# Where the weight tiles of 256-column products begin: 8 bytes instead of 64 behind a multiple of 512

## The chip, the cores and the metric

The kernel runs on one core of a Trainium2 chip. The metric is the time of one execution on the device in microseconds (us), the median of several runs. The engines are named as in the profile: PE is TensorE's matmul, PEld its weight load (which may run beside a matmul), DVE is VectorE, ACT is ScalarE, POOL is GpSimd, SP is SyncE.

## The reference

Two pre-norm residual layers over 512 tokens and 1024 channels, each with a mixer and a gated feed-forward block, all modulated by a conditioning vector; then a last norm. Everything is float32.

```python
for i in range(2):
    shift, scale, gate = adaln_params(c, ada_w[i, 0], ada_b[i, 0])
    hn = rmsnorm(h, norm_g[i, 0]) * (1.0 + scale) + shift
    m = s5_mixer(hn, ...) if i == 0 else fox_mixer(hn, ...)   # state space; causal attention, 16 heads
    h = h + gate * m
    shift, scale, gate = adaln_params(c, ada_w[i, 1], ada_b[i, 1])
    hn = rmsnorm(h, norm_g[i, 1]) * (1.0 + scale) + shift
    a, b = jnp.split(hn @ w_up, 2, axis=-1)                   # 1024 -> 2 x 2816
    h = h + gate * ((jax.nn.silu(causal_conv3(a)) * b) @ w_down)
return rmsnorm(h, final_g)
```

## The kernel before, in words

Channels lie on the 128 partitions and tokens along the free dimension, so a product multiplies a stationary 128x128 weight tile with a moving block of activations of up to 512 columns (tokens).

Each large product is done in three passes of a reduced float32 format. A value is split into a high part, rounded to that format, and the low rest (`put_parts`: ScalarE writes `w_hi`, VectorE subtracts and writes `w_lo`). `mms` (its matmul is lines 294 and 295) multiplies hi by hi, hi by lo and lo by hi into one PSUM sum. Every one of the three loads its 128x128 weights anew.

`product` handles a list of output tiles in up to three stages:

- `head`: the first tiles at once. For the two feed-forward layers it works in two halves of 256 tokens (`HALVES`), so that the first half can begin while the norm of the second is under way. The output product of the attention has a head too, with `halves=(slice(0, S),)`, one pass of 512.
- the middle: one output tile after the other over all 512 tokens.
- `tail`: the last 2 or 4 tiles again in halves of 256 tokens, so that the next norm's statistics of the first half can begin early. Tails stand in the state-space output product (moving `zhi`, `zlo`), both feed-forward down products (`ghi`, `glo`) and the attention's output product (`v`).

`quarters` makes most pairs of up-projection tiles by a scheme with seven products of half size instead of eight. Its inner function `times` (line 550) issues 4 x 3 matmuls of 256 columns for each of the seven, 84 for a pair, and 33 pairs in all. VectorE forms the sums of weight blocks (`sums`, line 518), `parts` splits them, and ScalarE and VectorE put the products together (`nm_h` line 557, `nm_t` line 518). Between pairs come pieces of the down product of the group before, over 512 columns on line 294.

Weight tiles come from `part_of`: a tile with 128 elements more than needed, whose contents begin `aside` elements behind the start. The pools are padded (`fill`) so that tiles begin at multiples of 512 bytes in a partition, and the 128x128 pieces of a tile are 512 bytes apart: what `aside` sets holds for every piece. Before, `aside` was 0 by default (heads, middles) and `ASIDE = 16` elements, 64 bytes, for tails, quarter products and the value products of the attention. In the value products (`fox_values`, matmul on line 1361) the weights are the moving operand and the activations the stationary one.

The order on each engine is that of the program text with a few added constraints; weight loads come over SyncE's queue, and a background task of the modulation weights (`ada_units`) uses POOL's queue and VectorE (line 247) during the first feed-forward layer.

Of the kernel before, what the change touches and what calls it, by code (L numbers as in the profile page):

```python
# [17 lines left out]
P = 128  # L18
# [40 lines left out]
def fill(pool, n):  # L59

    pool.tile([P, n // 4], F32, name="fill", bufs=1)


ROOM, ASIDE = 9 * P, 16


def part_of(pool, shape, name, tag, bufs, aside=0):
# [6 lines left out]
class Trunk:  # L74
# [223 lines left out]
    def product(self, w, ms, nk, x, evac, head=0, tail=0, after=None, ticks=0, halves=HALVES, tail_pool=(), first=None, step=None):  # L298


        ms = list(ms)
        full = slice(0, S)
        if head:
            wk = first or {m: self.weights(w[m], nk) for m in ms[:head]}
            ps = {m: self.mm.tile([P, S], F32, name="mmp") for m in ms[:head]}
            for c in halves:
                for k in range(nk):
                    for m in ms[:head]:
                        self.mms(ps[m][:, c], wk[m], x, k, nk, c)
                    self.finish_norm((k + 1) * head)  # L310
                    if step:
                        step(3)
            for m in ms[:head]:
                evac(m, ps[m], full)
                self.tick(ticks)
        for m in ms[head:len(ms) - tail]:
            wk = self.weights(w[m], nk)
            ps = self.mm.tile([P, S], F32, name="mmp")
            for k in range(nk):
                self.mms(ps, wk, x, k, nk, full)  # L320
                if step:
                    step()
            evac(m, ps, full)
            self.tick(ticks)
        if tail:
            last = ms[len(ms) - tail:]
            wk = {m: self.weights(w[m], nk, *tail_pool, aside=ASIDE) for m in last}
            for c in HALVES:
                for m in last:
                    if c is HALVES[1] and m == last[tail // 2]:  # L330
                        rb = self.rms_rows(y)
                    ps = self.mm.tile([P, S // 2], F32, name="mmp")
                    for k in range(nk):
                        self.mms(ps, wk[m], x, k, nk, c)
                    evac(m, ps, c)
                if c is HALVES[0]:
                    y = after[0](c)
                else:
                    y2 = after[0](c)
                    after[1](HALVES[0], y, rb)  # L340
            self.pending = lambda: after[1](HALVES[1], y2)
# [947 lines left out]
class Kernel(S5):  # L1289
# [32 lines left out]
    def fox_values(self, pool, x):  # L1322

        nc = self.nc

        self.v = pool.tile([P, KT, NB, 2, 2, HD], F32R, name="v")
        ft = pool.tile([P, NB, NH], F32, name="ft")
        fill(pool, 1792)
        bf = self.fox_bf
        W = VH * HD  # L1330
        xhi, xlo = x

        def load(qs):

            out = {q: [] for q in qs}
            for c in range(3):
                for q in qs:
                    src = self.io["fox_v"][q - 1] if q else self.io["fox_vf"]
                    n, step = (W, 4) if q else (W + NH, 3)
                    a = c * step  # L1340
                    j = min(step, KT - a)
                    if j <= 0:
                        continue
                    with self.behind(*(self.squared if 0 in qs and c else ())):
                        hi, lo = self.split(src[:, a:a + j, :], [P, j, n], aside=ASIDE)
                    out[q] += [(hi[:, i, :], lo[:, i, :]) for i in range(j)]
            return out

        def values(qs, blocks, w, aux=()):
            todo = [(q, b) for q in qs for b in blocks]  # L1350
            ps = {
                k: self.aux.tile([P, S], F32, name="aux") if k in aux else self.mm.tile([P, S], F32, name="mmp")
                for k in todo
            }
            for k in range(KT):
                for q, b in todo:
                    hi, lo = w[q][k]
                    n = W if q else W + NH
                    tb = slice(b * P, (b + 1) * P)
                    for i, (xt, wt) in enumerate(((xhi, hi), (xhi, lo), (xlo, hi))):  # L1360
                        self.last_mm = nc.tensor.matmul(  # L1361
                            ps[q, b][:, :n], xt[:, k, tb], wt, start=(k == 0 and i == 0), stop=(k == KT - 1 and i == 2),
                        )
                self.finish_norm((k + 1) * len(todo))
            for q, b in todo:
                pv = ps[q, b][:, :W].rearrange("p (g r d) -> p g r d", r=2, d=HD)
                hi, lo = (self.v[:, 2 * q:2 * q + 2, b, :, t, :] for t in range(2))
                self.evac = [self.put_parts(hi, lo, pv).ins]
                if todo[0][0] == 0 and (b != 1 or q):
                    self.tick(1)  # L1370
                if q == 0:
                    nc.vector.tensor_tensor(ft[:, b, :], ps[q, b][:, W:W + NH], bf, ALU.add)

        w = load(range(2))
        self.tick(1)
        values((0, 1), (0, 1), w)
        values((0, 1), (2, 3), w, ((0, 2), (0, 3)))
        lf = self.log_forget(ft, pool)
        for q in range(2, NV):
            values((q,), range(NB), load([q]))  # L1380
        return lf
# [259 lines left out]
```

## Time and profile before

| | |
|---|---|
| median of 3 runs | 1240.85 us (1239.77 to 1241.22) |
| profiled execution | 1233.09 us, span of its instructions 1231.3 us |
| granted TensorE clock | 0.995 of full speed |
| PE busy | 1200.5 us, 7921 matmuls |
| PEld busy | 1031.2 us, 7921 loads |
| DVE busy | 1009.0 us, 1872 instructions |
| ACT busy | 606.3 us, 1137 instructions |
| bytes moved by DMA | 183.83 MB |

The durations of matmuls are those of a pipelined engine: one may begin before the one before it has ended, so the time that a run of matmuls takes is read from the distance between starts. A row of a stretch gives for each engine the busy time in it and, in brackets, how many instructions began there.

### The profile page before, as it was taken

How to read it: one execution, taken by the hardware profiler on the slowest of the kernel's cores; microseconds unless marked ns; L12 is line 12 of the kernel's file. 1: busy time of each engine (PE TensorE's matmuls, PEld its weight loads, DVE VectorE, ACT ScalarE, POOL GpSimd, SP SyncE). 2: the span in 40 equal slices, each digit the busy share in tenths (PEclk: the TensorE clock that was granted, in tenths of full speed). 3: DMA queues.
4: the chain of work that ended last, by engine and by line, in shares of the span. 5: the costliest groups of instructions: out<-in, count | busy, mean ns of one | idle time of the engine just before them, and what ended most of it. 6: DMA issues, size and time to landing. Idle time of an engine off the chain costs nothing.

```text
span 1231.3 us, 20566 instructions
## 1 busy us (share of the span) xinstructions
PE 1200.5 (97%) x7921; PEld 1031.2 (84%) x7921; DVE 1009.0 (82%) x1872; ACT 606.3 (49%) x1137; POOL 82.7 (7%) x143
## 2 busy tenths in 40 slices
PE   7999999999999999999999999999999999999997
PEld 2466678898989899889899887878989999999987
DVE  7988886779899988799687578876899887888865
ACT  3543465335544543445443565664366554545443
POOL 0000000100000000000000243430000000000000
PEclk9999999999999999999999999999999999999999
DMA  9776668530354544444445543432122332323231
GB/s 356 244 237 215 223 225 286 192 129 35 129 178 158 192 161 160 152 168 132 125 139 190 176 150 124 147 118 94 70 69 95 120 122 77 116 86 123 95 96 69
DMA packets 74385, 183.83 MB, mean 149 GB/s; under 512 B 23231, under 2 KB 25631, under 8 KB 73263
## 3 DMA queue, kind: packets, MB, share of 16 engines
q1 hardware_dynamic: 68239, 161.02, 38.4%
q0 software_dynamic: 5760, 20.97, 5.0%
q8 instruction: 62, 1.02, 0.3%
q10 hardware_dynamic: 288, 0.52, 0.1%
q14 instruction: 36, 0.29, 0.1%
HBM read 175.57 MB, written 6.92 MB: 148 GB/s over the span
## 4 chain that ended last, share of the span: by engine, by line
PE 75%; DVE 15%; DMA 4%; issue 3%; ACT 2%; POOL 0%; SPq 0%; DVEq 0%; ACTq 0%; POOLq 0%
PE mmp L294 32%; PE mmp L550 16%; PE aux L550 6%; DVE w_lo L278 5%; PE mmp L1169 4%; PE mmp L1361 2%; DMA rawd<-in_w_down 2%; PE aux L971 2%; PE mmp L1198 2%; PE aux L1060 1%; PE aux L1500 1%; PE mmp L205 1%; PE aux L1052 1%; DVE ada_raw L247 1%; PE mmp L1109 1%
## 5 line engine op out<-in xcount | busy, mean ns | idle before, releaser
L278 DVE TENSOR_TENSOR w_lo<-raw,w_hi 128x1024 fp32r<-128x1024 f32 (+4 forms) x173 | 183.3, 1065 | 35.4 <-ACT w_hi L277 34.8
L277 ACT ACTIVATE w_hi<-raw 128x1024 fp32r<-128x1024 f32 (+4 forms) x173 | 154.8, 905 | 101.5 <-PE mmp L294 53.1
L294 PE MATMUL mmp<-ghi,w_hi 128*128 128x512 f32 (+1 forms) x392 | 145.1, 370 | 0.0
L294 PE MATMUL mmp<-glo,w_hi 128*128 128x512 f32 (+1 forms) x392 | 144.8, 369 | 0.0
L294 PE MATMUL mmp<-ghi,w_lo 128*128 128x512 f32 (+1 forms) x392 | 144.5, 369 | 0.0
L294 PE MATMUL mmp<-a_hi,w_hi 128*128 128x512 f32 (+1 forms) x376 | 138.8, 372 | 1.5 <-ACT a_hi L433 1.5
L294 PE MATMUL mmp<-a_hi,w_lo 128*128 128x512 f32 (+1 forms) x376 | 136.6, 364 | 0.3 <-DVE w_lo L278 0.3
L294 PE MATMUL mmp<-a_lo,w_hi 128*128 128x512 f32 (+1 forms) x376 | 136.2, 363 | 0.0
L550 PE MATMUL mmp<-w_hi 128*128 128x256 f32 x396 | 111.4, 281 | 2.6 <-ACT nm_h L557 2.6
L550 PE MATMUL mmp<-w_hi,w_lo 128*128 128x256 f32 x396 | 111.1, 281 | 0.7 <-DVE w_lo L278 0.7
L550 PE MATMUL mmp<-w_lo,w_hi 128*128 128x256 f32 x396 | 111.1, 281 | 0.0
L557 ACT ACTIVATE nm_h<-mmp 128x256 f32<-128x256 f32 x99 | 37.9, 384 | 131.5 <-PE mmp L550 131.5
L278 DVE TENSOR_TENSOR w_lo<-sums,w_hi 128x1024 fp32r<-128x1024 f32 x74 | 90.1, 1219 | 0.3 <-ACT w_hi L277 0.2
L294 PEld LDWEIGHTS mmp<-ghi,w_lo 128*128 128x128 f32 x392 | 74.2, 189 | 12.7 <-DVE w_lo L278 0.4
L294 PEld LDWEIGHTS mmp<-glo,w_hi 128*128 128x128 f32 x392 | 74.5, 190 | 11.1
L277 ACT ACTIVATE w_hi<-sums 128x1024 fp32r<-128x1024 f32 x74 | 76.7, 1054 | 14.4 <-DVE sums L518 11.2
L294 PEld LDWEIGHTS mmp<-ghi,w_hi 128*128 128x128 f32 x392 | 74.2, 189 | 11.4
L294 PEld LDWEIGHTS mmp<-a_hi,w_hi 128*128 128x128 f32 x376 | 70.6, 189 | 13.8 <-issue 2.6
L294 PEld LDWEIGHTS mmp<-a_hi,w_lo 128*128 128x128 f32 x376 | 70.9, 189 | 12.3 <-DVE w_lo L278 1.3
L362 DVE SCALAR_TENSOR_TENSOR h<-mmp,par,h 128x512 f32<-128x512 f32 (+1 forms) x100 | 68.1, 683 | 15.3 <-PE mmp L294 15.0
L294 PEld LDWEIGHTS mmp<-a_lo,w_hi 128*128 128x128 f32 x376 | 71.1, 189 | 9.7
L550 PEld LDWEIGHTS mmp<-w_hi 128*128 128x128 f32 x396 | 74.3, 188 | 3.0 <-ACT nm_h L557 3.0
(317 smaller groups left out, 3092.6 us busy)
## 6 DMA issues: line engine op xcount, KB each, us to landing
raw<-in_w_up SPq DMA_DIRECT2D x88, 512.0 KB, 3.3
raw<-in_ada_w SPq DMA_DIRECT2D x40, 512.0 KB, 6.3
ada_raw<-in_ada_t POOLq DMA_DIRECT2D x40, 512.0 KB, 3.9
nf<-nfd SPq DMA_DIRECT2D x8, 1152.0 KB, 6.5
raw<-in_fox_qk SPq DMA_DIRECT2D x16, 512.0 KB, 3.6
raw<-in_w_down SPq DMA_DIRECT2D x24, 320.0 KB, 3.0
rawd<-in_w_down SPq DMA_DIRECT2D x24, 256.0 KB, 3.4
raw<-in_w_down SPq DMA_DIRECT2D x16, 384.0 KB, 3.3
```

Source lines behind the costliest of these rows:

```text
L205: self.last_mm = nc.tensor.matmul(ps[32 * qq:32 * qq + 32, :], self.sc32[:, k, :], w[:, q * S:(q + 1) * S], start=(step is steps[0]), stop ...
L247: nc.vector.tensor_tensor_reduce(w, w, self.c_row, 1.0, 0.0, ALU.mult, ALU.add, sums[:, j:j + 1])
L277: nc.scalar.activation(hi, src, AF.Copy)
L278: return nc.vector.tensor_tensor(lo, src, hi.bitcast(F32), ALU.subtract)
L294: self.last_mm = self.nc.tensor.matmul(o, wt, xt[:, cols], start=(k == 0 and n == 0), stop=(k == nk - 1 and n == 2),)
L362: add = self.nc.vector.scalar_tensor_tensor(self.h[:, m, cols], ps, self.par[i][:, 16 + m:17 + m], self.h[:, m, cols], op0=ALU.mult, op1=A ...
L550: self.last_mm = nc.tensor.matmul(o, wt[:, k], xt[:, k], start=(first and k == 0 and n == 0), stop=(k == H - 1 and n == 2), skip_group_che ...
L557: a = nc.scalar.activation(t, o, AF.Copy)
L971: nc.tensor.matmul(ps[g2][:, j, cols], x[rows, a + j, r].rearrange("p c j -> p (c j)"), self.rr[rows, planes, q, :], start=(j == 0 and r = ...
L1169: nc.tensor.matmul(ps, w[m][:, k, :], x[:, k], start=(k == 0), stop=(k == KT - 1))
L1198: nc.tensor.matmul(gps[m], wt, xt[:, k], start=(k == 0 and part == 0 and xt is yhi), stop=(k == KT - 1 and part == 1))
L1361: self.last_mm = nc.tensor.matmul(ps[q, b][:, :n], xt[:, k, tb], wt, start=(k == 0 and i == 0), stop=(k == KT - 1 and i == 2),)
```

## The change

`ASIDE` becomes 2 elements (8 bytes). A new name `VALUES` keeps 16 elements for the attention's value products. Heads that work in two halves, those of the two feed-forward layers, get `ASIDE` as well; before they had 0. Tails and quarter products use `ASIDE` as before and so move from 64 to 8 bytes. No instruction is added, removed or reordered.

```diff
-ROOM, ASIDE = 9 * P, 16
+ROOM, ASIDE, VALUES = 9 * P, 2, 16
...
-            wk = first or {m: self.weights(w[m], nk) for m in ms[:head]}
+            wk = first or {m: self.weights(w[m], nk, aside=ASIDE if len(halves) == 2 else 0) for m in ms[:head]}
...
-                        hi, lo = self.split(src[:, a:a + j, :], [P, j, n], aside=ASIDE)
+                        hi, lo = self.split(src[:, a:a + j, :], [P, j, n], aside=VALUES)
```

## The prediction

> **What bounds the kernel now.** I read the page first: its engine busy times and the chain that ended last.
>
> ```profile
> span 1231.3 us, 20566 instructions
> PE 1200.5 (97%) x7921; PEld 1031.2 (84%) x7921; DVE 1009.0 (82%) x1872; ACT 606.3 (49%) x1137; POOL 82.7 (7%) x143
> PE 75%; DVE 15%; DMA 4%; issue 3%; ACT 2%; POOL 0%; SPq 0%; DVEq 0%; ACTq 0%; POOLq 0%
> ```
>
> TensorE is busy for 97% of the span and is three quarters of the chain. A nanosecond taken from each of thousands of matmuls shows in the time, as long as VectorE, at 82%, keeps up. The profiled execution took 1233.09 us (span 1231.3), 7.8 us below the median 1240.85; I carry differences over to the median.
>
> The next view is the stretches of line 550, the quarter products of the two feed-forward layers. Its columns are length, PE busy (instructions), weight loads, clock, DMA share, GB/s. Two rows of that line alone follow, with durations min/median/max.
>
> ```profile
> 300.00:605.00 305.00, 151.83 (x1260) 150.30 (x1260) 1.00 0.46 156
> 905.00:1190.00 285.00, 180.85 (x1512) 180.40 (x1512) 1.00 0.32 105
> ...
> L550 PEld LDWEIGHTS mmp<-w_hi x396: 186/188/189, 314.4 to 1183.0; 128*128 128x128 f32 x198
> L550 PE MATMUL mmp<-w_hi x396: 276/281/384, 314.6 to 1183.1; 128*128 128x256 f32 x198
> ```
>
> These 1260 + 1512 = 2772 matmuls occupy TensorE for 332.7 us. They follow one another faster than their recorded 281 ns, so the spacing of starts is what counts. It is read from the timeline of TensorE: start, duration, line. I show first and last rows of undisturbed stretches.
>
> ```profile
> 1036.05 0.28 PE L550 MATMUL mmp<-a_hi,w_hi 128*128 128x256 f32 x1
> ...
> 1045.94 0.40 PE L294 MATMUL mmp<-ghi,w_hi 128*128 128x512 f32 x1
> ...
> 365.73 0.28 PE L550 MATMUL mmp<-w_hi,w_lo 128*128 128x256 f32 x1
> 366.12 0.38 PE L550 MATMUL mmp<-a_hi,w_hi 128*128 128x256 f32 x1
> ...
> 366.58 0.28 PE L550 MATMUL mmp<-a_hi,w_hi 128*128 128x256 f32 x1
> ...
> 370.21 0.28 PE L550 MATMUL mmp<-w_hi,w_lo 128*128 128x256 f32 x1
> ...
> 279.75 0.28 PE L294 MATMUL mmp<-a_hi,w_hi 128*128 128x256 f32 x1
> ...
> 285.75 0.28 PE L294 MATMUL mmp<-a_hi,w_lo 128*128 128x256 f32 x1
> ...
> 427.91 0.39 PE L294 MATMUL mmp<-ghi,w_hi 128*128 128x512 f32 x1
> ...
> 430.86 0.39 PE L294 MATMUL mmp<-glo,w_hi 128*128 128x512 f32 x1
> ```
>
> - Weights at +64 bytes, undisturbed: 84 matmuls in 1045.94 - 1036.05 = 9.89 us, **117.7 ns** each.
> - The same line and offset after a wait in the middle of a group (at 365.73 the next start comes 0.39 us later): 32 steps in 3.63 us, **113.4 ns**.
> - Heads, weights at +0: 50 steps in 6.00 us, **120.0 ns**.
> - 512 columns: 13 steps in 2.95 us, 226.9 ns, twice 113.4. So 113.4 is what 256 columns cost at the rate of the wide products, and I take it for the floor.
>
> The reader is to see that a product over 256 columns costs 113.4, 117.7 or 120.0 ns at the same clock (granted 1.00 above) and in the same shape. Going through the starts of all 33 groups of 84 I count 2526 steps of 116 to 119 ns and 224 of 112 to 115. The median 281 in the row above says the same, since 276 is the duration at the fast spacing. The fast steps all lie behind a wait in four or five groups of the first layer.
>
> Two pairs of rows show what overlaps:
>
> ```profile
> 330.04 0.28 PE L550 MATMUL mmp<-w_lo,w_hi 128*128 128x256 f32 x1
> 330.04 0.19 PEld L550 LDWEIGHTS mmp<-w_hi,w_lo 128*128 128x128 f32 x1
> ...
> 330.16 0.28 PE L550 MATMUL mmp<-w_hi,w_lo 128*128 128x256 f32 x1
> 330.16 0.19 PEld L550 LDWEIGHTS mmp<-w_hi 128*128 128x128 f32 x1
> ```
>
> Each load starts with the matmul before the one that it serves, and runs beside that one's streaming. With 512 columns a load has 227 ns to hide in, with 256 only 113. The load is what the narrow product can be late for, and its address is what the change moves.
>
> **The change part by part.** It adds and removes no instruction, no transfer and no wait, and moves no step in any queue. It moves where the two parts of a weight tile begin.
>
> 1. *Quarter products, +64 to +8.* Between the floor and 117.7 lie 4.3 ns: 2526 x 4.3 = 10.9 us to be had. On the other side, at 120.0, the 2526 lose 2.3 ns (5.8 us) and the 224 fast ones 6.6 ns (1.5 us).
> 2. *Tails, +64 to +8, and heads of the feed-forward layers, +0 to +8.* Rows by shape, one for each product that has them:
>
> ```profile
> L294 PE MATMUL mmp<-a_hi,w_hi 128*128 128x256 f32 x96 | 27.2, 290 | 1.5 <-ACT a_hi L433 1.5
> L294 PE MATMUL mmp<-ghi,w_hi 128*128 128x256 f32 x80 | 23.3, 291 | 0.0
> L294 PE MATMUL mmp<-v,w_hi 128*128 128x256 f32 x64 | 11.6, 282 | 0.0
> L294 PE MATMUL mmp<-zhi,w_hi 128*128 128x256 f32 x32 | 9.2, 286 | 0.0
> ```
>
> Each stands for a third of its product, the v row for two thirds. Heads are 3 x 96 = 288 matmuls. About 250 run at the steady 120.0 and could gain 6.6 ns: 1.7 us. Tails are 240 + 96 + 96 = 432. By my count 310 run slow and 90 fast: 310 x 4.3 = 1.3 us to gain, or 310 x 2.3 + 90 x 6.6 = 1.3 us to lose.
>
> 3. *Fox values* keep +64 under a new name, and the head of the attention's output product has one pass of 512 columns and keeps 0. Nothing.
> 4. *The writers of the parts.* ScalarE and VectorE now write at +8. No row shows that offset. The nearest are the same copies at +0 (most of the raw row) and +64 (the sums row):
>
> ```profile
> L277 ACT ACTIVATE w_hi<-raw 128x1024 fp32r<-128x1024 f32 x97 | 101.9, 1056 | 68.5 <-PE mmp L294 43.5 <-PE mmp L1361 7.7 <-DMA raw<-in_w_up 7.6
> L277 ACT ACTIVATE w_hi<-sums 128x1024 fp32r<-128x1024 f32 x74 | 76.7, 1054 | 14.4 <-DVE sums L518 11.2 <-PE mmp L294 1.9 <-DVE sums L495 1.0
> ```
>
> 1056 against 1054 ns: the writer does not see the offset. I take nothing, with 2 ns on some 140 copies (0.3 us) as a bound both ways.
>
> *Which spacing at +8?* No row shows it; the ends are 113.4 and 120.0. By distance in bytes the nearest row is +0, by kind it is +64, the only other row in which load and stream do not begin at the same place of a 512-byte block. I go by how the three spacings behave. At +0 every long stretch ends at 120.0, also those that begin after a wait. At +64 the same tiles run at 117.7 or at 113.4 for a whole group, depending on how the group began. So what costs is a meeting of load and stream that, once in step, repeats itself in every matmul. At +0 it happens from the first column of the load on (the full 6.6 ns), at +64 from a third of the way on (4.3 of 6.6) or not at all. Eight bytes are two of 128 columns: the load crosses each boundary 2/128 of 113 ns, 1.8 ns, earlier than from +0. That should take it past the first meeting while staying far from the later one. I take the floor, and keep 120.0 as the other end; this is the weakest step.
>
> *What of the gain stays.* VectorE makes the parts and the sums for these products. Stretches (length, PE, loads, DVE, ACT, POOL, clock and DMA), and waits:
>
> ```profile
> 340.00:400.00 60.00, 59.88 (x386) 54.45 (x385) 56.23 (x90) 27.11 (x46) 4.24 (x8) 1.00 0.49 171
> 900.00:960.00 60.00, 60.00 (x408) 55.46 (x407) 57.67 (x81) 35.65 (x54) 0.00 (x0) 1.00 0.29 93
> 1020.00:1080.00 60.00, 60.00 (x430) 56.51 (x428) 48.27 (x74) 30.05 (x49) 0.00 (x0) 1.00 0.26 90
> ...
> PE mmp L550 <- ACT nm_h L557: 2.6, 2, 2.4
> ...
> DVE sums L518 <- DMA raw<-in_w_up: 12.9, 10, 2.9
> ```
>
> In the first layer VectorE is busy 56 of 60 us, and TensorE already waits for it in places, so I give back 40% of its share: 0.4 x 10.9 x 1260/2772 = 2.0 us. In the second it has 12 of 60 us free except at the start; I give back 15%, 0.9 us, and 0.3 us at heads and tails, which end in waits anyway. Sum: 10.9 + 1.7 + 1.3 - 3.2 = 10.7 us, or 1240.85 - 10.7 = **1230.1 us** (profiled execution 1222.4).
>
> [...]
>
> **The rivals.**
> - *Slower: +8 behaves as +0.* Place: every quarter and tail matmul; it decides from 117.7 ns on. Price: 5.8 + 1.5 + 1.3 = 8.6 us, heads unchanged: 1249.4. For it: nearness in bytes. Against: at +0 the meeting is exact, and two columns undo just that. Chance 0.20.
> - *One piece more per load.* If a load reads its 128 columns in pieces, and four columns are the smallest piece that a shift of two cuts, it needs 33 pieces instead of 32. That is 113/32 = 3.5 ns, an estimate: the floor becomes 116.9: 0.8 x 2526 = 2.0 us, heads 250 x 3.1 = 0.8, tails 0.2, together 3.0: 1237.9. For it: a narrow product's load has no slack at all. Against: at the floor it has, if the stream and not the load sets 113.4. Chance 0.10.
> - *No difference.* Load and stream may not see each other's addresses, +0 and +64 differing by how their groups are entered; then all stays at 1240.85. For it: the same tiles run at 113.4 and 117.7. Against: no head stretch holds 113. [...] A gain that VectorE takes back whole ends here too. Chance 0.15.
>
> **How the numbers follow.** The forecast has 0.55, with its own range 1226.5 (all 13.9 us stay) to 1235 (VectorE takes back half). 0.2% is 2.5 us, about what this measurement can tell from no change. Faster: 0.55 + 0.10 = 0.65; same 0.15; slower 0.20. Forecast, extra piece and no difference hold 0.80 up to 1243.3, less what of the forecast lies outside its own range, so the range reaches into the slower case: 1226.5 to 1249.
>
> **What would show it.** Right: the median of line 550 falls from 281 to 276 ns, a group of 84 takes 9.5 instead of 9.89 us, the heads' row falls from 290 towards 280, the 332.7 us of PE on line 550 become about 322, and line 550 waits more for nm_h and w_lo. Wrong: 120 ns in the groups (slower rival), 117 (the extra piece), or 113 in the groups with the span unmoved, VectorE then being the bound.

## The result and the profile after

| | before | after |
|---|---|---|
| median of 22 runs each | 1238.32 us (1233.17 to 1243.84) | 1230.99 us (1226.01 to 1241.19) |
| ratio after / before | | 0.9952, 95% interval 0.9935 to 0.9968 |

By the ratio the change takes 5.9 us off (0.48% of 1238.32; by the interval 4.0 to 8.0); the medians lie 7.3 us apart. The forecast was 10.7 us less: the sign was right, the size was not.

The page of the kernel after, the same three lines as of before:

```profile
span 1239.4 us, 20566 instructions
PE 1206.5 (97%) x7921; PEld 1032.6 (83%) x7921; DVE 1008.3 (81%) x1872; ACT 606.7 (49%) x1137; POOL 82.3 (7%) x143
PE 59%; issue 26%; DVE 8%; DMA 3%; POOL 2%; ACT 1%; SPq 0%; POOLq 0%; DVEq 0%; ACTq 0%
```

This profiled execution took 1241.19 us, the longest of the 22, and is longer than the profiled one of before (1233.09). So the two pages must not be subtracted. The reason stands in the first 100 us, where the change does nothing. The stretch 0 to 100 us, first of before, then of after (length, PE, loads, DVE, ACT, POOL, clock, DMA share, GB/s):

```profile
0.00:100.00 100.00, 91.02 (x588) 49.01 (x588) 85.24 (x258) 42.43 (x110) 1.32 (x20) 1.00 0.78 274
```

```profile
0.00:100.00 100.00, 91.78 (x521) 48.75 (x523) 79.63 (x247) 41.33 (x107) 1.31 (x20) 0.93 0.73 259
```

At a granted clock of 0.93 instead of 1.00, 521 instead of 588 matmuls began there. Over all profiles of this study the first 1400 matmuls took 200 to 210 us, with the old offsets and with the new. From here on I compare stages, each from a given matmul to another one by their order.

The views that the prediction named, of after. Line 550 alone in its two stretches, then two of its rows:

```profile
300.00:620.00 320.00, 152.03 (x1260) 150.31 (x1260) 0.99 0.47 152
915.00:1200.00 285.00, 177.66 (x1512) 177.25 (x1512) 1.00 0.34 106
```

```profile
L550 PEld LDWEIGHTS mmp<-w_hi x396: 186/188/331, 322.8 to 1191.2; 128*128 128x128 f32 x198
L550 PE MATMUL mmp<-w_hi x396: 277/279/415, 322.9 to 1191.3; 128*128 128x256 f32 x198
```

The timeline of a group of 84 in the second layer (first row, and the first row behind it), and of a head of the first layer:

```profile
1046.11 0.28 PE L550 MATMUL mmp<-a_hi,w_hi 128*128 128x256 f32 x1
...
1055.82 0.40 PE L294 MATMUL mmp<-ghi,w_hi 128*128 128x512 f32 x1
```

```profile
287.64 0.28 PE L294 MATMUL mmp<-a_hi,w_hi 128*128 128x256 f32 x1
...
294.00 0.28 PE L294 MATMUL mmp<-a_lo,w_hi 128*128 128x256 f32 x1
```

84 matmuls take 9.71 us, **115.6 ns** each; the head takes 6.36 us for 55 steps, 115.6 too. The starts repeat a pattern of 115, 115, 117 ns. Every undisturbed stretch of after has it, quarters, heads and tails, and also those that begin behind a wait. So three levels of before (120.0, 117.8 and 113.3) became one. They stand 2.2 ns apart: 113.3, 115.6, 117.8, 120.0.

What each stage took (us, worked out from the starts of the matmuls numbered 1720, 2000, 3700, 5600, 5760 and 7600), in two profiles of each kernel; the second ones are experiments e7 and e6 below:

| | before | before again | after | after again |
|---|---|---|---|---|
| head of the first feed-forward layer | 47.68 | 47.67 | 47.18 | 47.11 |
| its quarters, most of the down product between | 263.46 | 266.07 | 267.08 | 267.00 |
| head of the second | 29.25 | 29.25 | 28.96 | 28.99 |
| its quarters | 260.63 | 260.60 | 257.34 | 257.34 |
| from there to the end | 55.94 | 55.94 | 55.75 | 55.74 |

The second layer has 3.3 us less, both heads together 0.8, the end 0.2. The first layer's quarters have **nothing** less. That is 4.3 us in the stages of the table; the other 1.6 us lie inside the interval (4.0 to 8.0) and I can't place them. Two stretches are not in the table: up to matmul 1720 (266.8 and 271.9 us before, 275.6 and 268.5 after) and from 3700 to 5600 (307.6 and 307.3 before, 307.5 and 307.8 after). The other tails lie in them.

The rows by shape, and the wait that matters in the first layer (releaser, total us, count, longest):

```profile
L294 PE MATMUL mmp<-a_hi,w_hi 128*128 128x256 f32 x96 | 26.7, 285 | 1.5 <-ACT a_hi L433 1.5
L294 PE MATMUL mmp<-zhi,w_hi 128*128 128x256 f32 x32 | 9.1, 284 | 0.0
```

```profile
ACT w_hi L277 <- DMA rawd<-in_w_down: 40.5, 16, 6.7
```

In before the last row reads, between 300 and 620 us:

```profile
ACT w_hi L277 <- DMA rawd<-in_w_down: 34.5, 15, 5.1
```

`rawd` is the buffer of the down product's raw weights in the first layer (line 183). The prediction did not name it.

### The profile page after: what moved, and what is told of

It reads as the page before. It is cut to its first block, busy times and chain, and to the rows that moved or that the text cites. A ratio compares the mean times of both kernels' runs of the same rounds, so it can differ in the third digit from the quotient of the medians.

```text
span 1239.4 us, 20566 instructions
## 1 busy us (share of the span) xinstructions
PE 1206.5 (97%) x7921; PEld 1032.6 (83%) x7921; DVE 1008.3 (81%) x1872; ACT 606.7 (49%) x1137; POOL 82.3 (7%) x143
## 3 DMA queue, kind: packets, MB, share of 16 engines
q0 software_dynamic: 5760, 20.97, 5.2%
## 4 chain that ended last, share of the span: by engine, by line
PE 59%; issue 26%; DVE 8%; DMA 3%; POOL 2%; ACT 1%; SPq 0%; POOLq 0%; DVEq 0%; ACTq 0%
PE mmp L294 23%; PE mmp L550 11%; PE mmp L1169 5%; PE aux L550 4%; PE mmp L1361 2%; PE aux L971 2%; DVE w_lo L278 2%; PE mmp L1198 2%; POOL ada_raw L233 1%; PE aux L1060 1%; PE mmp L205 1%; PE aux L1500 1%; PE aux L1052 1%; DMA ada_raw<-in_ada_t 1%; PE mmp L1109 1%
```

## The experiments on the spacing

**Every pair of tiles with an offset of its own (e1).** One kernel, 33 groups, 31 offsets; the tile of weights is the same, only its beginning moves. The value products get 2 elements as well.

```diff
-ROOM, ASIDE, VALUES = 9 * P, 2, 16
+ROOM, ASIDE, VALUES = 9 * P, 2, 2
+SWEEP = (dict(...), dict(zip(range(4, 22), (2, 0, 1, 3, 4, 5, 6, 8, 10, 12, 14, 16, 18, 24, 32, 48, 64, 96))))
...
+        aside = SWEEP[l][f]
-                if where else part_of(self.wpool, [P, len(names) * H, P], n, n, WB, ASIDE)
+                if where else part_of(self.wpool, [P, len(names) * H, P], n, n, WB, aside)
```

> The changed kernel with another offset in each of the 33 groups of quarter products (first layer 2, 16, 7, 9, 11, 13, 15, 20, 28, 40, 80, 112, 120, 124, 126 elements of 4 bytes; second layer 2, 0, 1, 3, 4, 5, 6, 8, 10, 12, 14, 16, 18, 24, 32, 48, 64, 96), and the value products' moving weights at 8 bytes instead of 64. The computation is whole. What is read is the spacing of starts inside each group of 84 matmuls. Theory of the meeting: a meeting of load and stream costs 6.67 ns, and of each three passes 0, 1, 2 or 3 meet, so a group takes 9.52, 9.71, 9.89 or 10.08 us and nothing between; 0 takes 10.08, 16 takes 9.89, 2 takes 9.71, and an offset with 9.52 exists. Theory of the extra piece: every offset that is no multiple of 4 elements takes 9.71, every multiple of 4 takes 9.89 or 9.52, except 0. Value products: if only the distance between load and stream counts, moving weights at 8 bytes run at 115.6 ns, as quarter products do; if the load's own address counts, they keep 113.4 and 117.7.

Measured: 1237.78 us in one run (before beside it 1242.49). The timeline of the groups at offsets 0, 3 and 16 elements, each from its first row to the first row behind it, and a run of value products at 2:

```profile
933.67 0.28 PE L555 MATMUL mmp<-a_hi,w_hi 128*128 128x256 f32 x1
...
943.75 0.28 PE L555 MATMUL mmp<-a_hi,w_hi 128*128 128x256 f32 x1
...
957.79 0.28 PE L555 MATMUL mmp<-a_hi,w_hi 128*128 128x256 f32 x1
...
967.60 0.40 PE L298 MATMUL mmp<-ghi,w_hi 128*128 128x512 f32 x1
...
1083.47 0.28 PE L555 MATMUL mmp<-a_hi,w_hi 128*128 128x256 f32 x1
...
1093.37 0.40 PE L298 MATMUL mmp<-ghi,w_hi 128*128 128x512 f32 x1
...
661.77 0.28 PE L1366 MATMUL mmp<-w_hi,a_hi 128*128 128x256 f32 x1
...
664.53 0.28 PE L1366 MATMUL mmp<-w_hi,a_lo 128*128 128x256 f32 x1
```

10.08 us at 0, 9.81 at 3, 9.90 at 16; the value products run at 120.0 ns (23 steps in 2.76 us). All groups of the second layer, worked out in the same way (the first, at 2 elements, has wide products between, so its spacing of 115.7 ns is taken 84 times; the groups at 0 and 1 follow a narrow group, the others a wide product):

```
elements  0     1     2     3     4     5     6     8     10    12    14    16    18    24    32    48    64    96
us of 84  10.08 9.94  9.72  9.81  9.94  10.07 10.23 9.94  10.00 9.94  9.89  9.89  9.94  9.86  10.09 9.89  10.07 10.09
```

Two elements is the lowest of the 18, and both neighbours are dearer; the nine groups of the first layer that ran undisturbed, at other offsets, took 9.80 to 10.07. Neither theory of the spacing holds: levels lie in between (3 gives 116.8 ns), one above (6 gives 121.8), and offsets that are multiples of 16 bytes are not alike: 0 gives 120.0 ns, 4 elements 118.3, 16 117.8, 64 119.9. What does recur is a step of 64 elements, 256 bytes: 0 and 64 cost about the same, and so do 32 and 96 (120.1 ns each). In the value products the shift of 2 moves the *moving* operand, and 173 of their 288 steps lie at 120. So it isn't the distance between the two operands alone that decides; moving the load's beginning to 8 bytes helps, moving the stream's there does not. At 64 bytes, which both kernels keep for them, the value products change from run to run: of 273 steps 185 and 100 lie at 112 to 114 ns in the two profiles of before, 130 and 6 in those of after.

**Fewer columns (e2).** In the second layer each matmul of a pair but the one that opens a sum works on fewer columns, at offsets 0, 2 and 16.

```diff
+WIDTH = dict(zip(range(4, 22), ((d, n) for d in (0, 2, 16) for n in (256, 240, 224, 192, 128, 64))))
...
+                    c = slice(0, wide if k or n else N)
-                        o, wt[:, k], xt[:, k], start=...
+                        o[:, c], wt[:, k], xt[:, k, c], start=...
```

> The changed kernel; in the second layer's 18 groups of quarter products the offset is 0, 2 or 16 elements (six groups each), and all but the first pass of a product stream only 256, 240, 224, 192, 128 or 64 of the 256 columns. It leaves out the rest of those columns' sums. If the load sets the spacing of 120.0, 115.6 and 117.7 ns, narrower streams leave it where it is, down to the load's own time of about 108 to 113 ns, and the offset's difference stays at 240 columns. If the stream is what is slowed, the spacing falls with the columns: 240 columns take 15/16, 112.5, 108.3 and 110.3 ns, until the load binds.

Three groups of its timeline: 240 columns at offset 2, 128 columns at offset 0, 128 columns at offset 2.

```profile
1040.41 0.28 PE L553 MATMUL mmp<-a_hi,w_hi 128*128 128x256 f32 x1
...
1049.90 0.40 PE L295 MATMUL mmp<-ghi,w_hi 128*128 128x512 f32 x1
...
984.89 0.28 PE L553 MATMUL mmp<-a_hi,w_hi 128*128 128x256 f32 x1
...
994.26 0.45 PE L295 MATMUL mmp<-ghi,w_hi 128*128 128x512 f32 x1
...
1090.95 0.28 PE L553 MATMUL mmp<-a_hi,w_hi 128*128 128x256 f32 x1
...
1100.33 0.44 PE L295 MATMUL mmp<-ghi,w_hi 128*128 128x512 f32 x1
```

With half the columns a group still takes 9.37 us at offset 0 and 9.38 at 2, 111.5 ns a matmul: that is the load by itself, and its address is not seen. (The matmul that opens a sum has 256 columns and the one behind it starts 170 ns later, the next one 60 ns after that, but the loads go on about every 112 ns.) With 240 columns a group takes 9.49 at offset 2 and 9.53 at 16, about 113 ns. Only with 256 columns do the offsets part (9.72 at 2, 9.89 at 16). So neither expectation came whole: the load sets the spacing once the stream is narrower, as the first says, but the offset's difference is gone at 240 columns. (The kernel takes 1274.94 us, since TensorE waits 16.8 us for `nm_h` in the second layer and the clock drops in some groups; I read only undisturbed ones.) The load, at 111.5 ns, and the stream of 256 columns, at 113.3, have nearly the same period, and the loss of 2 to 8.5 ns was seen only there.

**The two parts at different offsets (e5).** hi and lo weights of a pair begin at offsets of their own.

```diff
+PAIRS = (dict(...), dict(zip(range(4, 22), [(2, 2), (13, 13), (80, 80), (2, 0), (0, 2), ...])))
...
+        pair = dict(zip(("w_hi", "w_lo"), PAIRS[l][f]))
-                if where else part_of(self.wpool, [P, len(names) * H, P], n, n, WB, ASIDE)
+                if where else part_of(self.wpool, [P, len(names) * H, P], n, n, WB, pair[n])
```

> The changed kernel with different offsets for the high and the low part of the weights in each group of quarter products, (high, low) in elements. First layer: (2,66) (66,2) (2,34) (34,2) (2,18) (18,2) (2,126) (126,2) (2,32) (32,2) (2,80) (80,2) (2,6) (3,3) (16,0). Second layer: (2,2) (13,13) (80,80) (2,0) (0,2) (2,16) (16,2) (2,4) (4,2) (2,1) (1,2) (2,3) (3,2) (2,64) (64,2) (2,10) (10,2) (17,17). The computation is whole. Theory that each load meets the stream by its own offset alone: two of three passes load the high part, so (2,x) stays within 1 ns of 115.6 for any x and (x,2) comes near the value of x, 120.0 for (0,2) and (64,2). Theory that one load shifts the start of the next, so that the three passes lock as one: (2,x) scatters from 113.4 to 120 like x itself. (13,13) and (80,80), which ran at 113.4 only behind a wait in the first layer, run without a wait here: at 113.4 if the offset does it, at about 118 to 120 if the wait did.

Measured (1236.01 us): (2,2) 115.6 ns; (2,0), (0,2), (2,64) and (64,2) all 117.8; (2,16) 116.7, (16,2) 117.8; (2,10) 118.8. One part at 2 and one at 0 is not two thirds of the one plus one third of the other (117.0 or 118.5), so a load does not meet the stream by its own offset alone. That the three passes settle into one rhythm together fits this, but (2,x) does not follow x either, and no run shows the locking by itself. Shifting one part by 64 elements more, (2,66) and (66,2), leaves 115.6, although 0 and 64 are both slow. And (13,13) and (80,80) came out at the floor:

```profile
933.98 0.28 PE L555 MATMUL mmp<-w_hi,w_lo 128*128 128x256 f32 x1
934.09 0.28 PE L555 MATMUL mmp<-a_hi,w_hi 128*128 128x256 f32 x1
...
943.61 0.28 PE L555 MATMUL mmp<-a_hi,w_hi 128*128 128x256 f32 x1
...
953.13 0.40 PE L298 MATMUL mmp<-ghi,w_hi 128*128 128x512 f32 x1
```

9.52 us each for 84, 113.3 ns. But the rows also show how the first one begins: 110 ns behind a matmul of 256 columns, the group before following without a wide product between.

**13 and 80 elements throughout (e8, e9).** Does the offset give the floor, or the start?

```diff
-ROOM, ASIDE, VALUES = 9 * P, 2, 16
+ROOM, ASIDE, VALUES = 9 * P, 13, 16      # e8; 80 in e9
```

> The changed kernel with 13 elements (52 bytes) instead of 2 for all its narrow products. In the experiment with pairs a group at (13,13) ran at 113.33 ns, but it began straight behind a group at 115.6. If the offset holds 113.33 from any start, groups take 9.52 us, heads 113.4 ns, the second layer (257.34 us from the 5600th-odd to the 7600th matmul at 8 bytes) gets 18 x 0.19 = 3.4 us shorter, and the time falls by a further 4 us against the changed kernel, to a ratio of about 0.992 to before. If the start decides, groups behind 512-column products take 9.7 to 10.1 us, and the time is that of the kernel before or up to 0.5% above.

> The same with 80 elements (320 bytes, a multiple of 64). Its group ran at 113.33 ns too, straight behind one at 113.33. If the offset decides: as for 13, ratio about 0.992. If the start decides, a multiple of 64 bytes with two states behaves as 64 bytes did, 117.8 ns, 9.89 us a group, and a ratio within 0.998 to 1.002.

A usual group of e8, behind a wide product, then of e9:

```profile
1040.12 0.39 PE L294 MATMUL mmp<-ghi,w_lo 128*128 128x512 f32 x1
1040.34 0.28 PE L550 MATMUL mmp<-a_hi,w_hi 128*128 128x256 f32 x1
...
1050.42 0.39 PE L294 MATMUL mmp<-ghi,w_hi 128*128 128x512 f32 x1
```

```profile
1035.43 0.28 PE L550 MATMUL mmp<-a_hi,w_hi 128*128 128x256 f32 x1
...
1045.33 0.40 PE L294 MATMUL mmp<-ghi,w_hi 128*128 128x512 f32 x1
```

The start. Behind a wide product 13 elements give 10.08 us (120.0 ns) and 80 give 9.90 (117.8, as 16 elements do, 256 bytes less). Within the groups of these two runs only matmuls that resume behind a wait run at 113.3, and not all of those: in e9 one group stays at 117.8 behind a wait of 0.9 us. The times follow: e8 1240.48 us, ratio to before 1.0028 (1.0005 to 1.0051); e9 1235.88, ratio 0.9989 (0.9964 to 1.0013). An offset thus has more than one rhythm, and how a stretch begins picks one. At its best, two elements (115.6 ns) is dearer than 13, 16 and 80 (113.3); of the offsets seen behind several starts (0, 2, 13, 16 and 80) it is the one that always stayed below 117.

## The experiments on the first layer

**Both kernels profiled again (e6, e7).** No edit. Is the missing gain of the first layer an accident of one execution?

> The changed kernel once more, for a second profile. Groups of quarter products without a wait take 9.71 or 9.72 us again. If the changed kernel's long first layer in the first profile (waits of 1.4, 1.0, 2.2 and 4.5 us in four groups) is a matter of the single run, the stretch from the first quarter product to the first of the value products differs from 319.0 us less its start by over 1 us; if it follows from the faster products, the same four groups wait as long.

> The kernel before once more, for a second profile: groups without a wait take 9.89 us again; the first 206 us and the waits of the first layer show how much one run differs from the next without any change.

Measured 1234.23 and 1240.45 us (before beside them 1239.27). The stages stand in the table above: the same groups of after are held up again, by 1.2, 1.1, 2.2, 4.6 and 0.6 us (numbers 2, 5, 10, 11 and 14, counted from 0), while nearly all others run at 9.72 us. Not all of the 4.6 us is waiting: behind a wait of 2.7 us some 16 starts lie 213 ns apart, at a granted clock of 0.60, and that is 1.6 us of it. The clock does not fall each time. The same group of the same kernel, before, waited 2.4 us in both profiles; the stretch behind the wait, first of before, then of before again:

```profile
537.50:541.00 3.50, 3.13 (x27) 3.13 (x28) 2.31 (x5) 2.04 (x6) 0.53 (x1) 1.00 0.58 186
```

```profile
544.00:548.00 4.00, 4.00 (x24) 4.00 (x24) 2.70 (x5) 2.27 (x3) 0.02 (x1) 0.61 0.59 199
```

This one group is 1.7 of the 2.6 us by which the two profiles of before differ in the table. The longest of the waits, in the timeline of e6:

```profile
535.19 0.68 DVE L278 TENSOR_TENSOR w_lo<-rawd,w_hi 128x512 fp32r<-128x512 f32 x1
535.90 5.56 SPq L183 DMA_DIRECT2D rawd<-in_w_down  x2
539.76 0.63 ACT L277 ACTIVATE w_hi<-rawd 128x512 fp32r<-128x512 f32 x1 [3.82 <-DMA rawd<-in_w_down]
540.29 0.64 ACT L557 ACTIVATE nm_h<-mmp 128x256 f32<-128x256 f32 x2
540.71 0.39 PE L550 MATMUL mmp<-w_hi 128*128 128x256 f32 x1 [2.68 <-ACT nm_h L557]
```

Read from the top: VectorE is the last reader of the one `rawd` buffer, at 535.19 for 0.68 us. Only then, at 535.90, may SyncE fetch the next one. ScalarE stands at its copy of it for 3.82 us, with `nm_h` of the quarters queued behind. TensorE needs `nm_h` to free a sum, and waits 2.68 us. The row on TensorE names `nm_h`; the cause is two steps further up, a buffer that exists once.

**Without the background task (e3 before, e4 after).** The task that makes the modulation of later layers during the first feed-forward layer is left out, its columns filled with a constant. It takes VectorE's time there (1.22 us for each instruction of line 247) and shares the DMA engines (20.97 MB on POOL's queue in the whole of before).

```diff
-        k.bg = [k.ada_units(units(*((2, t) for t in range(3)), (3, 2)))]
+        k.bg = []
+        for t in (k.par[2], k.par[3], k.ga[2]):
+            tc.nc.gpsimd.memset(t, 0.5)
```

> The kernel before without the background task of the modulation weights in the first feed-forward layer (its modulation columns are set to 0.5 instead, so the result is of other numbers). That frees 32 VectorE instructions of 1.22 us and 16 MB of transfers beside that layer. Read is the time from the first quarter product to the first value product. If VectorE and the transfers are what delays line 550 there, the waits inside its groups go from 5.6 us to near 0.

> The changed kernel without the same background task. If VectorE and the transfers took back the gain in the first layer, the stretch from the first quarter product to the first value product is now shorter than that of the kernel before without the task by the whole 15 x 0.18 = 2.7 us, plus 0.3 for the tail. If the gain is lost there for another reason, the two stretches stay within 1 us.

Of e4, the wait for the buffer, between 300 and 620 us:

```profile
ACT w_hi L277 <- DMA rawd<-in_w_down: 10.5, 9, 2.8
```

40.5 us became 10.5, and the groups run undisturbed. This pair can't tell which part of the task did it: without it VectorE, the last reader of the buffer, has less to do, and the transfers are faster (the median `rawd` transfer of 256 KB landed 2.7 instead of 3.4 us after its issue). The first layer's quarters take 258.09 us in e3 and 255.41 in e4: 2.68 us less, 15 groups x 0.18 us = 2.7. Yet the two differ by 2.0 us only (1228.62 and 1226.62), for two reasons. The first 1400 matmuls took 3.0 us longer in e4, as they vary anyhow. And the next stage, from matmul 3700 to 3990 with the first layer's tail, took 46.88 instead of 44.90. The waits of line 380 (the statistics of the next norm) between 300 and 640 us and the stretch behind them, of e3 and then of e4:

```profile
PE aux L380 <- DVE ssq L356: 1.4, 2, 1.0
...
614.00:622.00 8.00, 7.61 (x63) 7.24 (x62) 7.43 (x23) 2.88 (x7) 0.00 (x0) 1.00 0.54 166
```

```profile
PE aux L380 <- DVE ssq L356: 2.6, 2, 2.2
...
614.00:622.00 8.00, 8.00 (x58) 7.89 (x58) 6.12 (x20) 2.31 (x5) 0.00 (x0) 0.83 0.49 153
```

TensorE reached the norm earlier, waited 2.2 instead of 1.0 us for VectorE's sums of squares, and the granted clock behind that was 0.83 instead of 1.00. Here the gain that ended in a wait was given back and a little more.

**Two `rawd` buffers, the task kept (e10 before, e11 after).** If the buffer is the cause, a second one brings the gain back without touching VectorE's work. It takes the place of padding in the pool.

```diff
-            t = self.bgpool.tile(shape, F32, name=self.room, bufs=1)
+            t = self.bgpool.tile(shape, F32, name=self.room, bufs=2)
...
-            fill(pool, 1696)
+            fill(pool, 1696 if l else 160)
```

> The kernel before with two buffers instead of one for the first layer's down weights (rawd), and 1536 bytes less padding in that layer to make room. In the groups that begin with pieces of the down product, ScalarE waits up to 5 us for rawd with the copies nm_h behind it. If the single buffer is what those groups wait for, the waits inside the first layer's groups fall from 5.6 us (6.0 in its second profile) to under 2, and the stretch from the 2000th to the 3700th matmul from 263.5 and 266.1 us towards the 258.1 us of the kernel without the background task.

> The changed kernel with the same two buffers. If the single buffer took back the first layer's gain, that stretch falls from 267.0 us in both profiles to 2.5 us below that of the kernel before with two buffers. If VectorE's load took it, the stretch stays within 1 us of that kernel's.

No row of a wait for `rawd` is left in either. The first layer's quarters in the timeline, first of e10, then of e11:

```profile
317.10 0.28 PE L550 MATMUL mmp<-a_hi,w_lo 128*128 128x256 f32 x1
...
575.29 0.28 PE L550 MATMUL mmp<-a_lo,w_hi 128*128 128x256 f32 x1
```

```profile
313.33 0.28 PE L550 MATMUL mmp<-a_hi,w_lo 128*128 128x256 f32 x1
...
569.25 0.28 PE L550 MATMUL mmp<-a_lo,w_hi 128*128 128x256 f32 x1
```

258.19 and 255.92 us: the stretch is 5 to 8 us shorter for the old offsets and 11 us for the new ones, and between the two lie 2.27 us where with one buffer there was nothing. Single runs: 1227.63 and 1218.68. VectorE's work is as before (1007.4 and 1006.6 us busy). So VectorE's load alone does not hold the gain back; it did so through the single buffer, whose refill waits for VectorE's read. With the buffer doubled, or in e4 with less work and fewer transfers beside it, the gain is there.

**Both together, timed (e12).** The kernel of e11.

> The changed kernel with two buffers for rawd, timed. If the first layer's stretch is shorter by the 11.1 us seen in the two profiles (267.0 to 255.9), and nothing else moves by more than the 1.2 us that the second layer took longer there, the time is 5.9 + 11.1 - 1.2 = 15.8 us below the kernel before, a ratio of 0.987. If a single profile misled, the ratio lies nearer the changed kernel's 0.9952.

Measured 1220.68 us (1218.11 to 1224.13), ratio to before 0.9855 (0.9821 to 0.9889): 17.8 us less. Its page and a stretch of the first layer:

```profile
span 1219.2 us, 20580 instructions
PE 1193.1 (98%) x7921; PEld 1024.7 (84%) x7921; DVE 1007.5 (83%) x1872; ACT 609.2 (50%) x1137; POOL 82.3 (7%) x143
...
340.00:400.00 60.00, 60.00 (x390) 54.68 (x389) 55.00 (x88) 28.36 (x46) 4.22 (x8) 1.00 0.48 162
```

TensorE is busy for all 60 us of that stretch, with VectorE at 55. The time lies below that of both kernels.

## Why the prediction was right and where it was wrong

- *What bounds the kernel: right.* Spacing shows in the time where nothing else is waited for: 18 groups x 0.18 us = 3.24 us, and the second layer's quarters fell by 3.26 to 3.29.
- *"I take the floor, and keep 120.0 as the other end": the step that failed.* The spacing at +8 is 115.6 ns, not 113.4. For the quarters that halves the gain: 2526 x 2.2 = 5.6 us instead of 10.9, and the 224 matmuls that ran at 113.4 lose 2.2 ns, 0.5 us. The marks for it were named: a median of 276 ns for line 550 (it is 279), 9.5 us for a group (9.71), 332.7 us falling to 322 (152.03 + 177.66 = 329.7). The reason given, that two columns take the load past one meeting and leave it far from the next, does not hold: offsets of 3 and 4 elements should then do as well, and they give 116.8 and 118.3.
- *Heads: right in kind.* 120.0 became 115.6 and the row of 290 ns 285. The term of 1.7 us measured 0.8.
- *Tails.* 1.3 us was the term. The one that can be read alone, at the end, gave 0.2. Those that had run at 113 behind a wait lost what the others won.
- *What stays of the gain: near in sum by luck, wrong in cause and place.* The prediction gave back 40% in the first layer and 15% in the second, to VectorE, 3.2 us with the 0.3 us at heads and tails. The first gave back all of its 2.7 us, the second none. The row that was shown for "TensorE already waits for it" names ScalarE's `nm_h` (2.6 us), not VectorE. It was the single `rawd` buffer and the order on ScalarE, which the prediction did not price: it looked at the share of busy time, 56 of 60 us on VectorE, and not at which wait ends last. With two buffers the same VectorE lets 2.27 of 2.7 us through. That the forecast of 1230.1 us lies 0.9 us from the measured median is luck too: the median of before came out 2.5 us lower over 22 runs, and the gain is smaller than the forecast's.
- *The writers at nothing:* no run of mine measured the copies alone; DVE 1008.3 against 1009.0 us and ACT 606.7 against 606.3 show no cost.
- *The slower rival* did not come at 8 bytes. Its spacing exists: at 13 elements the groups run at 120.0 ns and the kernel is slower by 0.28% (e8).
- *The extra piece* gave a number close to the truth (116.9 ns) for a wrong reason. No run shows a load that reads in pieces; the pieces were supposed and their 3.5 ns estimated. If pieces of four elements set the price, offsets 4, 16 and 64 would be as good as 0 and 2 would be dearer than all; in e1 the four cost 118.3, 117.8, 119.9 and 120.0 ns, and 2 is the cheapest. Its sum of 3.0 us also leaves out the 224 fast matmuls, which would have lost 3.5 ns each, 0.8 us. Nor does e1 show any order by multiples of four: 115.6 to 121.8 ns at offsets that are none (2 and 6 elements), 117.4 to 120.1 at ones that are (24 and 32).
- *No difference*, because load and stream don't see each other's addresses, did not come: e1 alone has 115.6 to 121.8 ns by the address. With 512 columns the spacing in before is 226.9 ns, twice 113.4, with a load beside each, and at 240 columns e2 shows no difference between offsets (about 113 ns); at 256 the same pair of instructions costs 113.3 to 121.8 ns, and no run shows what it is that is lost there.

What stays open: why an offset gives the rhythm it gives. The runs show that the loss comes where the two periods are nearly equal (256 columns, and neither 240 nor 512), that the passes don't act each for itself (e5: 117.8 ns where a mix of two spacings would give 117.0 or 118.5), and that the start picks among rhythms. They don't show what it is that load and stream meet at. Nor are the 1.6 us between the stages and the ratio placed.

## What to carry to other kernels

Where a weight load and a stream take nearly the same time (here 111.5 and 113.3 ns), read the spacing of starts, not the durations, and try several beginnings of the tile in one kernel, each behind the start that it has in use. Before counting on a faster TensorE, find the wait that ends last in each stage and follow it up to its cause; here a buffer that exists once, behind a queue in order, took the gain of a layer back whole while VectorE was busy for 56 of 60 us.

## What the runs showed of the hardware

- The spacing of 256-column products in this format moves between 113.3 (before, e5) and 121.8 ns (e1) with the address of the weight tile and the start of the stretch, and of the offsets tried behind a wide product the best begins 8 bytes behind a multiple of 512 (115.6 ns, after).
- Offsets 256 bytes apart had the same spacing behind a wide product: 128 and 384 bytes 120.1 ns each (e1), 64 and 320 bytes 117.8 (before and e9).
- The same instructions at the same offset keep one of two rhythms for a long stretch, up to a whole group of 84 (at 13 elements 113.3 ns in e5 and 120.0 in e8), by how it began.
- With streams of 128 columns a matmul and its weight load repeat every 111.5 ns at offset 0 (9.37 us for 84) as at 2 (9.38) in e2; with 256 columns the lowest spacing of a stretch was 113.3 ns.
- Behind some waits on TensorE the granted clock was lower, and the length of the wait alone does not tell: 1.0 us was followed by a granted clock of 1.00 (e3) and 2.2 us by 0.83 (e4), but 2.4 us at one and the same place by 1.00 in one run of the kernel before and by 0.61 in the other.
